# The recurrence's small products of two heads issued as one run per level, into one PSUM bank

## The chip, the cores and the metric

One core of one Trainium2 chip. The metric is the device time of one launch in microseconds; 912.33 us is the median of three runs of the kernel before (911.7, 912.37, 912.33). The engines are named as the profile names them: PE (TensorE, with its weight loads as PEld), DVE (VectorE), ACT (ScalarE), POOL (GpSimd), SP (SyncE, which issues the DMAs).

## The reference

A transformer block on 512 rows of width 1024: one input projection feeds three branches (A: attention over selected keys with a learned bias per distance, B: a gated linear recurrence with 4 heads, C: latent attention), whose outputs are gated, added and projected, and a gated feed-forward layer follows. The change touches branch B alone:

```python
# per head, key width 128, value width 128; f is the gate, k = (1-lb)*sigmoid(-f_raw)
b = cumsum(log f)                      # inside a chunk
decay[t, s] = exp(b[t] - b[s]) for s <= t, else 0
attn[t, s] = sum_k q[t,k] * k[s,k] * decay[t,s,k]
o = attn @ v + (q * exp(b)) @ state
state = exp(b_last) * state + (k * exp(b_last - b)).T @ v
o = rms_norm(o, out_gain) * silu(g)
```

Since the decay depends on the key channel, `attn` is no single product. The kernel builds it by doubling: for two neighbouring blocks of `hh` rows, the later block's queries times the earlier block's keys is one small product, if the queries carry the gates since the start of their block and the keys the gates up to the end of theirs.

## The kernel before

The kernel is written as a list of operations that a planner orders. `Plan.add` (line 167) records each operation with the buffers that it reads and writes; `Plan.run` (232) then walks through a simulated time, gives each engine the operation that can start first (ties go to the one written first), with costs from `Plan.cost` (204), and assigns tiles to buffer slots; `Plan.emit` (319) issues everything in that order. Every instruction therefore has one and the same line, 323, in the profile, and its tile's names tell what it is. Within an engine the order is fixed when the program is built. `SLACK` (26) adds 500 ns in that simulated time before PE takes what another engine made. Work marked `background` (773) is taken only where nothing else is ready: above all the bias of branch A (`bias_unit`, 719), which DVE and ACT build by selecting among leaves (tile `mux`), and its mask (`block_mask`, 757).

The recurrence is `hgrn_pair` (910), called for heads (0, 1) and (2, 3). Per head it holds the queries `qT` (named `qp` in the levels), the keys `kT`, the gates `fT`, the products of neighbouring gates `tt`, the blocks on the diagonal `ac` and the whole 128x128 triangles of four chunks, `at`. First come the 16 products of 32x32 that give the diagonal. Then seven levels, `hh` = 1, 2, ..., 64. Each level, for each head by itself:

- takes a bank of tag `t` (`LIMIT`: three at a time) and issues the level's small products into it: 16 of 32x16 (levels 1 to 16), 8 of 32x32 (level 32) or 4 of 64x64 (level 64). Each product uses a strip of 32 or 64 columns of the array, and its result stands in the matching partitions. An fp32 product shows as two records in the profile;
- merges the result: for `hh` < 32 with a masked copy on DVE into `ac`, for 32 and 64 with copies on ACT into `at`;
- multiplies half of the queries and half of the keys by the level's gates (two DVE products of 128x256), so that the next level can start.

Other work on PE at that time is large products of 128x512 (the next projections: `ps<-hT_hi,whi` and the like), which the planner puts between the runs. After the recurrence come the gates and upward projections of branches C and B (`branch`, 1045, with `oc` and `ob`), then the attention of branch A, which needs the bias.

Of the kernel before, what the change touches and what calls it, by code (L numbers as in the profile page):

```python
# [143 lines left out]
class Plan:  # L144
# [22 lines left out]
    def add(self, choices):  # L167
        op = Op()
        op.choices, op.prio = choices, self.shift + len(self.ops)
        op.deps, op.users, op.ready, op.bufs, op.late = set(), [], 0.0, [], 0  # L170
        _, method, a, k = choices[0]
        args = list(a) + list(k.values())
        outs = [k[n] for n in ("out", "accum_out") if n in k]
        if "out" not in k:
            outs.append(a[0])
        for v in args:
            if not isinstance(v, View):
                continue
            write = any(v is o for o in outs)
            b = v.buf  # L180
            mask = 0
            for i in np.unique(v.idx // 64) if b.cls != "bank" else (0,):
                mask |= 1 << int(i)
            keep = []
            for other, m, w in b.log:
                if m & mask and (write or w) and other is not op:
                    op.deps.add(other)
                if not (write and m | mask == mask):
                    keep.append((other, m, w))
            keep.append((op, mask, write))  # L190
            b.log = keep
            if b not in op.bufs:
                op.bufs.append(b)
                b.left += 1
        if self.gate:
            op.deps.add(self.gate)
        for d in op.deps:
            d.users.append(op)
        op.late = len(op.deps)
        self.ops.append(op)  # L200
        return op

    @staticmethod
    def cost(engine, method, a, k):
        views = [v for v in list(a) + list(k.values()) if isinstance(v, View)]
        if method == "dma_start":
            n = max(v.idx.size for v in views)
            return n * 512 / 360.0
        n = max(v.idx.size for v in views)
        psum = any(v.buf.cls == "bank" for v in views)  # L210
        if engine == "PE":
            rhs = a[2]
            n = rhs.idx.size
            if method == "transpose":
                return 109.0
            if rhs.buf.dt == F32R:
                return n / 2.4 + 3 if n >= 256 else n * 4 / 2.4
            return n * 4 / 2.4
        if engine == "ACT":
            return n / 1.2 + (52 if psum else 93) + 93 * sum(isinstance(k.get(x), View) for x in ("scale", "bias")) + (92 if "accum_out" in k else 0)  # L220
        if engine == "DVE":
            if method == "reciprocal":
                return n * 8 / 0.96 + 68
            one = method in ("tensor_copy", "tensor_scalar") and not psum
            return n / (1.92 if one else 0.96) + 68 + (60 if method == "scalar_tensor_tensor" else 0)
        if method == "tensor_tensor" and k.get("op") == ALU.pow:
            return 165.0 * n + 300
        if method == "tensor_scalar":
            return n * 2.5 + 176 if k["op0"] in (ALU.is_le, ALU.is_equal, ALU.is_ge) else n * 0.832 + 162
        return n * 2.105 + 147  # L230
# [88 lines left out]
    def emit(self, nc):  # L319
        real = {"PE": nc.tensor, "DVE": nc.vector, "ACT": nc.scalar, "Pool": nc.gpsimd, "SP": nc.sync}  # L320
        fix = lambda v: v.real() if isinstance(v, View) else v
        for op, (e, method, a, k) in self.run():
            getattr(real[e], method)(*[fix(v) for v in a], **{n: fix(v) for n, v in k.items()})  # L323


@with_exitstack
def block_kernel(ctx: ExitStack, tc: tile.TileContext, x, positions, w_in, w_up_a, w_up_b, w_up_c, w_out, mla_q_norm,
                 mla_w_qb, mla_kv_norm, mla_w_kvb, hgrn_lb_logits, hgrn_out_norm, rel_bias, attn_norm, ffn_norm,
                 w_ffn_gate, w_ffn_up, w_ffn_down, final_norm, consts_f, consts_i, out):
    nc = tc.nc  # L330
# [5 lines left out]
    plan = Plan(slots)  # L336
# [7 lines left out]
    def g(shape=(128, 512), dt=F32, name="g"):  # L344
        return plan.tile("g", shape[1:], dt, name)
# [228 lines left out]
    ci = const((5, 16), I8, "ci")  # L574
# [332 lines left out]
    rows_group([(src(C_BG, 512), 0)], 512, put5)  # L907
    obT = (o8(name="ob_hi"), o8(name="ob_lo"))

    def hgrn_pair(hs):  # L910
        qp, at, ac, tt_ = {}, {}, {}, {}
        for h in hs:

            at[h] = g((128, 4, 128), name="at")
            P.memset(at[h], 0.0)
            ac[h] = g((128, 4, 32), name="ac")
            pd = bank("t", (128, 4, 32))
            for c in range(4):
                for i in range(4):
                    m = 128 * c + 32 * i  # L920
                    PE.matmul(pd[:, c].part(32 * i, 32 * i + 32), kT[h][:, m:m + 32], qT[h][:, m:m + 32], start=True,
                              stop=True)
            V.tensor_mul(ac[h], pd, id32.to_broadcast([128, 4, 32]))
            qp[h] = qT[h]
            V.tensor_mul(qp[h], qT[h], fT[h])
            tt_[h] = g(name="tt")
            f2 = fT[h].rearrange("p (n two) -> p n two", two=2)
            V.tensor_mul(tt_[h][:, 0:256], f2[:, :, 0], f2[:, :, 1])
            o = 0
            n = 256  # L930
            while n > 4:
                a = tt_[h][:, o:o + n].rearrange("p (n two) -> p n two", two=2)
                V.tensor_mul(tt_[h][:, o + n:o + n + n // 2], a[:, :, 0], a[:, :, 1])
                o += n
                n //= 2
        for lv in range(7):
            hh = 1 << lv
            for h in hs:
                pl = bank("t", (128, 4, 16 if hh < 32 else 64))
                if hh == 64:  # L940
                    for c in range(4):
                        s, m = 64 * (c % 2), 128 * c
                        PE.matmul(pl[:, c].part(s, s + 64), kT[h][:, m:m + 64], qp[h][:, m + 64:m + 128], start=True,
                                  stop=True)
                    for e in range(2):
                        A.copy(at[h][:, e:4:2, 64:128].part(0, 64), pl[:, e:4:2].part(64 * e, 64 * e + 64))
                elif hh == 32:
                    for c in range(4):
                        for s in (0, 64):
                            m = 128 * c + s  # L950
                            PE.matmul(pl[:, c, 0:32].part(s, s + 32), kT[h][:, m:m + 32], qp[h][:, m + 32:m + 64],
                                      start=True, stop=True)
                    for s in (0, 64):
                        A.copy(at[h][:, :, s + 32:s + 64].part(s, s + 32), pl[:, :, 0:32].part(s, s + 32))
                else:
                    for c in range(4):
                        for i in range(4):
                            m = 128 * c + 32 * i
                            q2 = qp[h][:, m:m + 32].rearrange("p (n two e) -> p n two e", two=2, e=hh)[:, :, 1]
                            PE.matmul(pl[:, c].part(32 * i, 32 * i + 32), kT[h][:, m:m + 32], q2, start=True, stop=True)  # L960
                    a2 = ac[h].rearrange("p c (n two e) -> p c n two e", two=2, e=hh)[:, :, :, 1]
                    m2 = ci[:, lv:lv + 1].to_broadcast([128, 4, 16]).rearrange("p c (n e) -> p c n e", e=hh)
                    V.copy_predicated(a2, m2, pl.rearrange("p c (n e) -> p c n e", e=hh))
                    if hh == 16:
                        for i in range(4):
                            ii = slice(32 * i, 32 * i + 32)
                            A.copy(at[h][:, :, ii].part(32 * i, 32 * i + 32), ac[h].part(32 * i, 32 * i + 32))
                if hh == 1:
                    tv = fT[h].rearrange("p (n two) -> p n two", two=2)
                else:  # L970
                    o = 512 - 1024 // hh
                    tv = tt_[h][:, o:o + 512 // hh].rearrange("p (n two) -> p n two", two=2)
                qv = qp[h].rearrange("p (n two e) -> p n two e", two=2, e=hh)
                kv = kT[h].rearrange("p (n two e) -> p n two e", two=2, e=hh)
                nn = 256 // hh
                V.tensor_mul(qv[:, :, 1], qv[:, :, 1], tv[:, :, 0:1].to_broadcast([128, nn, hh]))
                V.tensor_mul(kv[:, :, 0], kv[:, :, 0], tv[:, :, 1:2].to_broadcast([128, nn, hh]))
        for h in hs:
            hc = slice(h * 128, (h + 1) * 128)
            pk = bank("t", (128, 4, 128))  # L980
# [339 lines left out]
```

## Time and profile before

| what | value |
|---|---|
| median of three runs | 912.33 us |
| the profiled execution | 910.3 us |
| its span, first to last instruction | 908.5 us |
| mean granted TensorE clock | 0.995 |
| PE busy | 895.1 us, 99% |
| PEld busy | 777.6 us, 86% |
| DVE busy | 695.6 us, 77% |
| ACT busy | 521.5 us, 57% |

The profiled execution is one launch recorded by the hardware; its span leaves out 1.8 us around the instructions. PE and PEld overlap, as do PE's own records: a large product's record lasts 0.39 us, but the next one starts 0.23 us later. What a product costs is therefore read from one start to the next.

### The profile page before, as it was taken

To read this page: it belongs to the slowest core of one execution; us is meant where nothing else is said; L and a number is where in the kernel's file an instruction comes from. 1 tells how busy PE (TensorE), PEld (TensorE's weight loads), DVE (VectorE), ACT (ScalarE), POOL (GpSimd) and SP (SyncE) were. 2 spreads that over 40 slices of the span, in tenths; PEclk is the share of its full clock that TensorE was granted. 3 is DMA by queue.
4 is the path that set the end of the run, shared out by engine and by line. 5 is a ranking of instruction groups with operands and counts; after the bars stand their busy time and mean duration, and the time that the engine had idled before them with its cause. 6 is when DMAs were issued, how large, how long until landed. Compare 5 with 4: busy or idle time off the path is not lost.

```text
span 908.5 us, 15211 instructions
## 1 busy us (share of the span) xinstructions
PE 895.1 (99%) x5870; PEld 777.6 (86%) x5870; DVE 695.6 (77%) x1428; ACT 521.5 (57%) x985; POOL 20.9 (2%) x31
## 2 busy tenths in 40 slices
PE   7999999999999999999999999999999999999996
PEld 7988878886778888887888879999999999888885
DVE  5576999999999999997353448889998899844205
ACT  7656684496858798977742336554544454533103
POOL 2000000000102000000000000000000000000000
PEclk8999999999999999999999999999999999999999
DMA  8333122331122233143032551323333334643102
GB/s 266 81 93 99 48 70 65 99 92 50 48 72 71 69 115 117 47 139 94 1 103 83 176 172 48 117 70 94 97 115 115 93 94 128 177 138 114 47 1 92
DMA packets 76809, 86.53 MB, mean 95 GB/s; under 512 B 8385, under 2 KB 63809, under 8 KB 76737
## 3 DMA queue, kind: packets, MB, share of 16 engines
q1 hardware_dynamic: 76736, 85.57, 31.2%
q8 instruction: 46, 0.75, 0.3%
q14 instruction: 27, 0.21, 0.1%
HBM read 83.46 MB, written 2.10 MB: 94 GB/s over the span
## 4 chain that ended last, share of the span: by engine, by line
PE 92%; DMA 3%; DVE 2%; ACT 1%; issue 1%; SPq 0%; POOLq 0%; POOL 0%; ACTq 0%
PE ps L323 92%; DMA raw<-in_w_ffn_up 1%; DMA raw<-in_w_in 1%; DVE wlo L323 1%; DMA x2b<-in_x 1%; ACT whi L323 1%; DMA raw<-in_w_out 1%; SPq L323 0%; DVE qpT L323 0%; ACT qpT L323 0%; ACT L323 0%; DVE ckT_lo L323 0%; ACT sm L323 0%; DVE kpo L323 0%; DVE qpr L323 0%
## 5 line engine op out<-in xcount | busy, mean ns | idle before, releaser
L323 DVE TENSOR_TENSOR wlo<-raw,whi 128x1024 fp32r<-128x1024 f32 (+3 forms) x115 | 133.1, 1178 | 66.9 <-ACT whi L323 43.8
L323 ACT CAST whi<-raw 128x1024 fp32r<-128x1024 f32 (+3 forms) x115 | 115.1, 1016 | 91.1 <-PE ps L323 28.0
L323 PE MATMUL ps<-hT_hi,whi 128*128 128x512 f32 x328 | 130.9, 399 | 0.0
L323 PE MATMUL ps<-hT_hi,wlo 128*128 128x512 f32 x328 | 129.9, 397 | 0.0
L323 PE MATMUL ps<-hT_lo,whi 128*128 128x512 f32 x328 | 129.4, 395 | 0.0
L323 ACT ACTIVATE mux<-bucket,rb,rbd 128x512 f32<-128x512 f32 (+1 forms) x161 | 108.3, 743 | 11.0 <-DVE bucket L323 4.7
L323 DVE COPY_PREDICATED mux<-bits,mux 128x512 f32<-128x512 int8 x150 | 104.3, 744 | 0.7 <-ACT mux L323 0.6
L323 PE MATMUL ps<-th,sh 128*128 128x256 f32 x288 | 81.5, 283 | 0.0
L323 PE MATMUL ps<-tl,sh 128*128 128x256 f32 x288 | 81.5, 283 | 0.0
L323 PE MATMUL ps<-th,sl 128*128 128x256 f32 x288 | 81.5, 283 | 0.0
L323 ACT CAST sh<-sf 128x512 fp32r<-128x512 f32 x72 | 44.2, 621 | 51.9 <-DVE sf L323 30.0
L323 PEld LDWEIGHTS ps<-hT_hi,wlo 128*128 128x128 f32 x328 | 61.6, 188 | 12.2
L323 PEld LDWEIGHTS ps<-hT_lo,whi 128*128 128x128 f32 x328 | 61.7, 188 | 12.1
L323 PEld LDWEIGHTS ps<-hT_hi,whi 128*128 128x128 f32 x328 | 61.7, 188 | 12.0
L323 PE MATMUL ps<-whi,ah 128*128 128x512 f32 x176 | 68.5, 389 | 0.0
L323 PE MATMUL ps<-wlo,ah 128*128 128x512 f32 x176 | 68.5, 389 | 0.0
L323 PE MATMUL ps<-whi,al 128*128 128x512 f32 x176 | 68.5, 389 | 0.0
L323 PE MATMUL ps<-h_hi,sl 128*128 128x256 f32 x216 | 61.1, 283 | 0.0
L323 PE MATMUL ps<-h_lo,sh 128*128 128x256 f32 x216 | 61.1, 283 | 0.0
L323 PE MATMUL ps<-h_hi,sh 128*128 128x256 f32 x216 | 61.1, 283 | 0.0
L323 PE MATMUL ps<-whi,hT_hi 128*128 128x512 f32 (+3 forms) x160 | 54.2, 345 | 1.4 <-ACT hT_hi L323 1.4
L323 PEld LDWEIGHTS ps<-th,sh 128*128 128x128 f32 x288 | 55.3, 192 | 0.0
(313 smaller groups left out, 2118.2 us busy)
## 6 DMA issues: line engine op xcount, KB each, us to landing
raw<-in_w_in SPq DMA_DIRECT2D x51, 512.0 KB, 4.2
raw<-in_w_ffn_down SPq DMA_DIRECT2D x22, 512.0 KB, 4.3
raw<-in_w_ffn_gate SPq DMA_DIRECT2D x18, 512.0 KB, 3.7
raw<-in_w_ffn_up SPq DMA_DIRECT2D x18, 512.0 KB, 3.7
raw<-in_w_out SPq DMA_DIRECT2D x8, 512.0 KB, 3.9
raw<-in_w_up_c SPq DMA_DIRECT2D x4, 512.0 KB, 3.6
raw<-in_w_up_b SPq DMA_DIRECT2D x4, 512.0 KB, 3.7
raw<-in_w_up_a SPq DMA_DIRECT2D x4, 512.0 KB, 3.6
```

Source lines behind the costliest of these rows:

```text
L323: getattr(real[e], method)(*[fix(v) for v in a], **{n: fix(v) for n, v in k.items()})
```

## The change

The 16 diagonal products and the first level's of both heads go into one bank as one operation of the planner, and each later level's products of both heads into one bank as one operation. The two heads share one `ac` tile of (8, 32), so the masked copy of a level (and the diagonal's multiplication by the identity) is one DVE instruction for both. The queries get a tile of their own (`qp`) instead of being multiplied in place, because the first run reads both forms. The products of neighbouring gates (`tt`) are built a level at a time, at the end of each level, instead of all at the start. The planner's cost of such an operation is 310 + 9 x (number of products) ns.

```diff
@@ Plan.add, Plan.cost, Plan.emit
-        outs = [k[n] for n in ("out", "accum_out") if n in k]
-        if "out" not in k:
+        outs = [k[n] for n in ("out", "accum_out") if n in k] + k.get("outs", [])
+        args += k.get("outs", [])
+        if "out" not in k and "outs" not in k:
             outs.append(a[0])
...
+        if method == "batch":
+            return 310.0 + 9.0 * len(k["outs"])
...
+            if method == "batch":
+                k["body"](nc, *[fix(v) for v in a], *[fix(v) for v in k["outs"]])
+                continue
@@ hgrn_pair
+    def batch(nc, *v):
+        n = len(v) // 3
+        for i in range(n):
+            nc.tensor.matmul(v[2 * n + i], v[i], v[n + i], start=True, stop=True)
+
     def hgrn_pair(hs):
-        qp, at, ac, tt_ = {}, {}, {}, {}
+        at, tt_, qp = {}, {}, {}
+
+        ac = g((128, 8, 32), name="ac")
         for h in hs:
...
-            ac[h] = g((128, 4, 32), name="ac")
-            pd = bank("t", (128, 4, 32))
-            for c in range(4):
-                for i in range(4):
-                    m = 128 * c + 32 * i
-                    PE.matmul(pd[:, c].part(32 * i, 32 * i + 32), kT[h][:, m:m + 32], qT[h][:, m:m + 32], start=True,
-                              stop=True)
-            V.tensor_mul(ac[h], pd, id32.to_broadcast([128, 4, 32]))
-            qp[h] = qT[h]
+            qp[h] = g(name="qp")
             V.tensor_mul(qp[h], qT[h], fT[h])
...
-            o = 0
-            n = 256
-            while n > 4:
-                a = tt_[h][:, o:o + n].rearrange("p (n two) -> p n two", two=2)
-                V.tensor_mul(tt_[h][:, o + n:o + n + n // 2], a[:, :, 0], a[:, :, 1])
-                o += n
-                n //= 2
+        def strips(width, parts):
+            pl = bank("t", (128, 8, width))
+            l, r, o = [], [], []
+            for e, h in enumerate(hs):
+                for rows, cols, a, b in parts(h):
+                    for c in range(4):
+                        for i, (ka_, qb) in enumerate(zip(a(c), b(c))):
+                            n = rows(c, i)
+                            l.append(ka_)
+                            r.append(qb)
+                            o.append(pl[:, 4 * e + c, cols].part(*n))
+            plan.add([("PE", "batch", l + r, {"outs": o, "body": batch})])
+            return pl
...
         for lv in range(7):
             hh = 1 << lv
-            for h in hs:
-                pl = bank("t", (128, 4, 16 if hh < 32 else 64))
...
+            else:
+                w = 0 if lv else 32
+                first = lambda h: [] if lv else [(quarter, slice(0, 32), chunks(kT[h], 32), chunks(qT[h], 32))]
+                pl = strips(w + 16, lambda h: first(h) + [(quarter, slice(w, w + 16), chunks(kT[h], 32),
+                                                           odd(qp[h], hh))])
+                if not lv:
+                    V.tensor_mul(ac, pl[:, :, 0:32], id32.to_broadcast([128, 8, 32]))
+                a2 = ac.rearrange("p c (n two e) -> p c n two e", two=2, e=hh)[:, :, :, 1]
+                m2 = ci[:, lv:lv + 1].to_broadcast([128, 8, 16]).rearrange("p c (n e) -> p c n e", e=hh)
+                V.copy_predicated(a2, m2, pl[:, :, w:w + 16].rearrange("p c (n e) -> p c n e", e=hh))
+            for n, h in enumerate(hs):
...
                 V.tensor_mul(qv[:, :, 1], qv[:, :, 1], tv[:, :, 0:1].to_broadcast([128, nn, hh]))
                 V.tensor_mul(kv[:, :, 0], kv[:, :, 0], tv[:, :, 1:2].to_broadcast([128, nn, hh]))
+                if 0 < hh < 64:
+                    o, n2 = 512 - 512 // hh, 256 // hh
+                    if n2 > 4:
+                        a = tt_[h][:, o:o + n2].rearrange("p (n two) -> p n two", two=2)
+                        V.tensor_mul(tt_[h][:, o + n2:o + n2 + n2 // 2], a[:, :, 0], a[:, :, 1])
```

Levels 32 and 64 (left out above) go through `strips` in the same way, with the copies on ACT unchanged.

## Rows read from the trace of the kernel before

**Rows 1.** The page's first part: busy us, share of the span, instructions.

```profile
PE 895.1 (99%) x5870; PEld 777.6 (86%) x5870; DVE 695.6 (77%) x1428; ACT 521.5 (57%) x985; POOL 20.9 (2%) x31
```

**Rows 2.** The chain that ended last, its share of the span by engine.

```profile
PE 92%; DMA 3%; DVE 2%; ACT 1%; issue 1%; SPq 0%; POOLq 0%; POOL 0%; ACTq 0%
```

**Rows 3.** Windows: from:to, length, busy us (instructions) per engine, clock, DMA share, GB/s.

```profile
207.29:229.43 22.14, 22.14 (x483) 14.76 (x481) 21.13 (x55) 14.16 (x29) 0.00 (x0) 1.00 0.17 50
300.00:400.00 100.00, 100.00 (x443) 82.76 (x442) 98.18 (x163) 92.70 (x142) 0.00 (x0) 1.00 0.31 95
400.00:415.00 15.00, 15.00 (x68) 12.42 (x67) 14.90 (x30) 8.27 (x11) 0.00 (x0) 1.00 0.20 70
```

**Rows 4.** Groups by shape, PE: the small products. After the bar busy us, mean ns.

```profile
L323 PE MATMUL ps<-qT,kT 128*32 128x16 f32 x640 | 8.9, 185 | 0.0
L323 PE MATMUL ps<-qT,kT 128*32 128x32 f32 x192 | 4.1, 199 | 0.0
L323 PE MATMUL ps<-qT,kT 128*64 128x64 f32 x32 | 1.8, 234 | 0.0
```

**Rows 5.** Timeline of PE around one level's run: start, length, what, records.

```profile
212.06 0.39 PE L323 MATMUL ps<-hT_hi,whi 128*128 128x512 f32 x1
212.28 0.40 PE L323 MATMUL ps<-hT_lo,whi 128*128 128x512 f32 x1
212.52 0.40 PE L323 MATMUL ps<-hT_hi,wlo 128*128 128x512 f32 x1
212.84 0.44 PE L323 MATMUL ps<-qT,kT 128*32 128x16 f32 x32
213.22 0.50 PE L323 MATMUL ps<-hT_hi,whi 128*128 128x512 f32 x1
213.55 0.40 PE L323 MATMUL ps<-hT_lo,whi 128*128 128x512 f32 x1
```

**Rows 6.** Timeline of PE around runs of levels 32 and 64.

```profile
267.05 0.39 PE L323 MATMUL ps<-hT_hi,wlo 128*128 128x512 f32 x1
267.37 0.45 PE L323 MATMUL ps<-qT,kT 128*32 128x32 f32 x16
267.75 0.50 PE L323 MATMUL ps<-hT_hi,whi 128*128 128x512 f32 x1
268.18 0.45 PE L323 MATMUL ps<-qT,kT 128*64 128x64 f32 x8
268.56 0.50 PE L323 MATMUL ps<-hT_lo,whi 128*128 128x512 f32 x1
268.90 0.39 PE L323 MATMUL ps<-hT_hi,wlo 128*128 128x512 f32 x1
```

**Rows 7.** Timeline of PE: two runs with one large product between.

```profile
259.42 0.45 PE L323 MATMUL ps<-qT,kT 128*32 128x16 f32 x32
259.80 0.50 PE L323 MATMUL ps<-hT_hi,wlo 128*128 128x512 f32 x1
260.23 0.45 PE L323 MATMUL ps<-qT,kT 128*32 128x16 f32 x32
```

**Rows 8.** Waits, 205 to 280 us: who for whom, us in total, times, longest.

```profile
PEld ps L323 <- issue: 8.0, 23, 0.4
PEld ps L323 <- DVE kT L323: 0.7, 2, 0.4
```

**Rows 9.** Groups by shape, DVE, 205 to 275 us; last, idle before and its releaser.

```profile
L323 DVE TENSOR_TENSOR qT<-qT,tt 128x256 f32<-128x256 f32 x24 | 10.1, 419 | 0.3 <-PE ps L323 0.2
L323 DVE COPY_PREDICATED ac<-ci,ps 128x64 f32<-128x64 int8 x20 | 5.0, 257 | 2.3 <-PE ps L323 2.0
L323 DVE TENSOR_TENSOR ac<-ps,id 128x128 f32<-128x128 f32 x4 | 1.2, 296 | 0.0
```

**Rows 10.** Timeline of DVE: the last mask added to branch A's bias.

```profile
414.54 0.68 DVE L323 TENSOR_TENSOR mux<-mux,neg 128x512 f32<-128x512 f32 x1
```

**Rows 11.** Timeline of PE: where the attention of branch A takes over.

```profile
420.19 0.49 PE L323 MATMUL ps<-ident,sm 128*128 128x128 f32 x3
```

More of the change, by code (lines that the diff above doesn't have):

```diff
@@ L936, in hgrn_pair, with chunks, odd @@
+        def chunks(v, n, o=0, step=1):
+            return lambda c: [v[:, m:m + n] for m in range(128 * c + o, 128 * c + 128, n * step)]
+        def odd(v, hh):
+            return lambda c: [v[:, m:m + 32].rearrange("p (n two e) -> p n two e", two=2, e=hh)[:, :, 1]
+                              for m in range(128 * c, 128 * c + 128, 32)]
+        quarter = lambda c, i: (32 * i, 32 * i + 32)
         for lv in range(7):
             hh = 1 << lv
-            for h in hs:
-                pl = bank("t", (128, 4, 16 if hh < 32 else 64))
[L940 to L944, printed above, removed]
-                    for e in range(2):
[L946 to L952, printed above, removed]
-                    for s in (0, 64):
[L954 to L967, printed above, removed]
@@ new lines, in hgrn_pair @@
+            if hh == 64:
+                pl = strips(64, lambda h: [(lambda c, i: (64 * (c % 2), 64 * (c % 2) + 64), slice(0, 64),
+                                            chunks(kT[h], 64, 0, 2), chunks(qp[h], 64, 64, 2))])
+                for n, h in enumerate(hs):
+                    for e in range(2):
+                        A.copy(at[h][:, e:4:2, 64:128].part(0, 64), pl[:, 4 * n + e:4 * n + 4:2].part(64 * e, 64 * e + 64))
+            elif hh == 32:
+                pl = strips(64, lambda h: [(lambda c, i: (64 * i, 64 * i + 32), slice(0, 32),
+                                            chunks(kT[h], 32, 0, 2), chunks(qp[h], 32, 32, 2))])
+                for n, h in enumerate(hs):
+                    for s in (0, 64):
+                        A.copy(at[h][:, :, s + 32:s + 64].part(s, s + 32), pl[:, 4 * n:4 * n + 4, 0:32].part(s, s + 32))
+            else:
[8 more added lines that the diff above has]
+                V.copy_predicated(a2, m2, pl[:, :, w:w + 16].rearrange("p c (n e) -> p c n e", e=hh))
@@ L968, in hgrn_pair @@
+            for n, h in enumerate(hs):
+                if hh == 16:
+                    for i in range(4):
+                        ii = slice(32 * i, 32 * i + 32)
+                        A.copy(at[h][:, :, ii].part(32 * i, 32 * i + 32), ac[:, 4 * n:4 * n + 4].part(32 * i, 32 * i + 32))
                 if hh == 1:
```

## The prediction

> **What bounds the kernel now.** First the shares: PE is busy 99% of the span [rows 1], and the chain that ended last is PE for 92% [rows 2]. A busy PE says little by itself, so the second look is at windows. The reader is to see the PE column equal to the length of the stretch: all of 22.14 us where the first pair's recurrence runs, all of the 100 us from 300 to 400, all of the 15 us after [rows 3]. In these stretches PE always has a next instruction, so what shortens PE's own stream shortens the kernel, as long as nobody else becomes late. The third look is at the small products. They have 864 records [rows 4], which is 432 products with two records each; per pair of heads they are 2 diagonals and 7 levels for 2 heads, so 16 runs, 32 runs in all. The groups' busy times, 8.9 + 4.1 + 1.8 = 14.8 us, leave out what surrounds a run; the price has to be read from starts.
>
> **One run's price.** Large products start 0.23 us apart (212.06 to 212.52, two steps). From 212.52, the last large product before a run, to 213.55, the second after it, are 1.03 us [rows 5]. Two large steps are 0.46, so the run costs 0.57 us. Where it goes: the first small product starts 0.32 after the large one instead of 0.23; the run's starts spread over 0.44 less one record's own 0.185, so 0.26 us for 31 steps, 8.3 ns each; PE leaves it 0.12 after its last start; and the first large product behind it is followed after 0.33 to 0.34 instead of 0.23. More than half is paid at the two ends. The short runs show it too: one of 16 records and one of 8 with one large product between them take from 267.05 to 268.90, 1.85 us, less three large steps 1.16, 0.58 each [rows 6], though the second has a quarter of the records of a level run. Their steps are longer, (0.45 - 0.20)/15 = 16.7 ns and (0.45 - 0.23)/7 = 31 ns. As a check, the window of the first pair holds 424 small records and about 58 large products that start in it: 22.14 - 58 x 0.23 = 8.8 us for 15 runs, 0.59 each [rows 3].
>
> **What is removed and added on PE.** Per pair the 16 runs become 7: the diagonals and the first level of both heads one run of 128 records, levels 2 to 16 four runs of 64, level 32 one of 32, level 64 one of 16. The count of products is the same. By steps: 0.57 + 96 x 0.0083 = 1.37; 4 x (0.57 + 32 x 0.0083) = 3.34; 0.58 + 16 x 0.0167 = 0.85; 0.58 + 8 x 0.031 = 0.83. Together 6.4 us, where 16 runs took 9.2 to 9.3. Two pairs: 2 x 2.85 = **5.7 us off PE's stream**. The unknown here is the step beyond the 32nd record of a run, since no run before is longer. Taking 8.3 ns I choose the nearest row; the slow end is the first rival.
>
> **DVE and ACT.** Ten masked copies of 128x64 pairs and two of `ac` multiplications become half as many with twice the elements: 12 instructions fewer. The step from 128x128 to 128x256 is 296 to 419 ns, so one twice as long saves at most 2 x 296 - 419 = 173 ns, and for the copies no more than their 257 [rows 9]: between 0 and 3 us, I take 1. The products with the gates, those of neighbouring gates and ACT's copies are the same in number; the latter products only move to the ends of levels, into DVE's stream between the same neighbours, without a DMA or another queue. The extra tile for the queries is paid by the shared `ac` and by `qT`, which is free after the first run. No DMA is added or moved past another; SP's order stays.
>
> **The wait that changes.** Before, a head's run waited for that head's two DVE products while the other head's were under way; now a run waits for all four, and DVE's next products wait for the end of the whole run, because they overwrite what it reads. PE has large products to fill this: its true waits at the recurrence are 0.7 us in two for `kT`, and the 8.0 us in 23 with no releaser are the runs' own entries [rows 8]. DVE's waits for such a run were 2.0 us [rows 9]; with a run of 0.84 instead of 0.57 us, and the planner's 310 + 9 x 32 = 598 ns for it, the filling that the planner picks is short by 0.24 a level. Twelve levels: up to 3 us more of idle DVE, at least none. It hits no PE work there, since two pairs' later projections and all of branch C's gates stand behind.
>
> **What is late next.** Branch A's bias is the other long work: from 300 to 400 us DVE is busy 98.18 and ACT 92.70 of 100, from 400 to 415 DVE 14.90 of 15 [rows 3]. Its last mask is added at 414.54 + 0.68 = 415.2 [rows 10], and PE turns to that attention at 420.19 [rows 11]. So PE can come 5.0 us earlier before it meets unfinished bias; it will come 5.7 earlier. DVE's own end moves by -1 to +3 us. What is lost there lies between 0 and all 5.7; early blocks of that attention and gates of branch A can fill, so I take 1.0. Net 4.7. Against the profiled execution: 910.3 - 4.7 = 905.6; the median of the runs lies 2.0 above that execution, so the forecast is **907.6 us**. Its own range is 905.5 to 910.
>
> **Rival 1, slower: long runs starve.** Until 32 records everything of a run may stand ready in PE before it begins; beyond, instructions have to be brought in while it runs. The rows allow a slow rate: from 259.42 two runs with one large product end their starts at 260.23 + 0.26, 1.07 us [rows 7]. If the first 32 were ready, the 33 behind them came in at 32 ns each or faster. Beyond the 32nd record lie 96 + 4 x 32 = 224 per pair, 448 in all. At 32 ns these cost 448 x (32 - 8.3) = 10.6 us more, less 5.7: 912.3 + 4.9 = **917.2 us**. It turns the sign from 8.3 + 5700/448 = 21 ns. For it: nothing shows a longer run. Against it: two runs so close together cost 0.58 each as well [rows 6], and a run with 8 records as much as one with 32, so no supply limit shows yet.
>
> The Trainium skill has a rule on this side ("TensorE: Matmul & The Clock Gate", section "Wait — 56ns, not 53.3ns?"): however small a product, the next one starts no less than about 25 ns later. Worked out from that figure, 32 more records would cost 0.80 us, more than the 0.57 that a run's ends and body cost, and the estimate for the change would be about 2 us slower. Inside a run this trace shows 8.3 ns, since neighbouring products use different strips, so the page's floor does not hold there; beyond the 32nd record no run here shows it.
>
> **Rival 2, no change: the bias holds it up.** PE arrives early at an attention whose bias isn't ready, and stands until it is. For it: the slack of 5.0 us is smaller than the gain, and DVE and ACT have no air for 100 us. Against it: PE has filled every such place so far. If DVE ends 1 us later and nothing fills, PE gains 5.0 - 1 = 4.0 less the way of the first blocks through DVE and ACT, which is 3 to 4 us of the present 5.0: some 0.5 us stay, **911.8**.
>
> **Rival 3: PE waits inside the runs.** If at each of the 12 later runs the fourth DVE product is late by its own 0.42 us [rows 9], PE loses 12 x 0.42 = 5.0 and the sum is 912.3 - 5.7 + 5.0 = **911.6**. Against it: PE is slower than the planner assumes (0.23 for a large product charged at 216 ns), so DVE tends to be early.
>
> **Chances.** Forecast 0.60; rival 1 0.16, of which some part would be a smaller loss or even a small gain; rival 2 0.14; rival 3 0.05; a new order that moves some other wait, either way, 0.05. About 0.2% of the time, 1.8 us, can be told from no change. Faster: the forecast, and the weak forms of rivals 1 and 3 and of the new order, 0.71. Same: rivals 2 and 3 in the main, 0.14. Slower: rival 1 and the rest, 0.15. The range reaches from 904.5 (all of 5.7, DVE's relief and 1 us of luck) to 914.0, which takes in rivals 2 and 3 and rival 1 with a step of some 25 ns; a full rival 1 is left out.
>
> **What would show it.** Right: 14 runs with 128, 64, 32 and 16 records; a run of 64 with starts spread over some 0.53 us; 0.84 us from large product to large product for it, above the two steps; from the first run to the last of a pair about the same time as before with more large products in it; PE full from 200 to 420. Rival 1: steps that lengthen behind the 32nd record. Rival 2: PE idle, or waiting for `sm` or `pT`, where the attention of branch A starts, with DVE's last mask close to 415. Rival 3: waits of PE for `qp` or `kT` at most runs. The forecast is wrong if PE's small work falls by 5 to 6 us and the time doesn't follow, or if it doesn't fall.

## The result, and the profile after

The changed kernel takes **906.91 us** (median of four, 906.78 to 907.51) against 912.35 for the kernel before on the same chip: a ratio of 0.9942, with a 95% interval from 0.9925 to 0.9959, or 5.4 us. The forecast was 907.6. Medians here and below leave out one slow execution, of the changed kernel with half of the background work, which took 2282.09 us.

The page of the changed kernel, its busy times:

```profile
PE 890.4 (98%) x5870; PEld 778.1 (86%) x5870; DVE 694.4 (77%) x1417; ACT 520.3 (57%) x983; POOL 19.7 (2%) x31
```

PE's records are 5870 as before, and it is busy 4.7 us less [rows 1]. Its span is 905.0 us against 908.5: 3.5 shorter, so PE stands 1.2 us longer than before. The windows show where (columns as in [rows 3]):

```profile
212.04:235.43 23.39, 23.39 (x494) 18.31 (x493) 20.10 (x53) 13.28 (x27) 0.00 (x0) 1.00 0.33 92
300.00:400.00 100.00, 100.00 (x443) 82.65 (x442) 97.52 (x161) 81.54 (x121) 0.00 (x0) 1.00 0.33 97
400.00:415.00 15.00, 15.00 (x70) 12.40 (x68) 15.00 (x27) 11.65 (x21) 0.00 (x0) 1.00 0.24 69
415.00:451.00 36.00, 34.77 (x204) 28.11 (x203) 21.26 (x85) 30.09 (x74) 0.00 (x0) 1.00 0.17 55
```

The reader is to see the last line: 34.77 of 36.00, the only stretch from 200 to 500 us in which PE isn't full. The first line is the first pair's recurrence up to its last run: 494 records, of which 416 small in six runs and some 77 large that start in it, so 23.39 - 77 x 0.23 = 5.7 us for six runs; before, 15 runs took 8.8 in [rows 3].

One level's run, PE's timeline (start, length, what, records), to be held against [rows 5]:

```profile
216.44 0.39 PE L329 MATMUL ps<-hT_hi,wlo 128*128 128x512 f32 x1
216.76 0.74 PE L919 MATMUL ps<-qp,kT 128*32 128x16 f32 x64
217.43 0.50 PE L329 MATMUL ps<-hT_hi,whi 128*128 128x512 f32 x1
217.76 0.39 PE L329 MATMUL ps<-hT_lo,whi 128*128 128x512 f32 x1
```

From 216.44 to 217.76 are 1.32 us, less two large steps 0.86. The entry is 0.32 and the step behind the first large product 0.33, as before; only the middle is longer, (0.74 - 0.185)/63 = 8.8 ns a record. The first run of a pair, its inner lines left out:

```profile
212.04 0.39 PE L329 MATMUL ps<-hT_lo,whi 128*128 128x512 f32 x1
212.36 0.46 PE L919 MATMUL ps<-qT,kT 128*32 128x32 f32 x32
...
213.21 0.43 PE L919 MATMUL ps<-qp,kT 128*32 128x16 f32 x30
213.57 0.50 PE L329 MATMUL ps<-hT_hi,wlo 128*128 128x512 f32 x1
213.91 0.39 PE L329 MATMUL ps<-hT_hi,whi 128*128 128x512 f32 x1
```

128 records cost 1.87 - 0.46 = 1.41 us. DVE in the recurrence, its groups by shape and then its longest waits:

```profile
L329 DVE COPY_PREDICATED ac<-ci,ps 128x128 f32<-128x128 int8 x10 | 3.6, 359 | 1.8 <-PE ps L919 1.7
L329 DVE TENSOR_TENSOR ac<-ps,id 128x256 f32<-128x256 f32 x2 | 0.8, 420 | 0.5 <-PE ps L919 0.5
```

```profile
DVE qp L329 <- PE ps L919: 2.5, 2, 1.8
DVE ac L329 <- PE ps L919: 2.2, 5, 0.9
```

A copy for both heads takes 359 ns where two took 2 x 257. The waits for runs add up to 4.7 us, against the 2.2 of [rows 9]. Of the 2.5 more, 1.8 are one wait, at the last level of the first pair.

Where PE stands, its timeline with the idle time in brackets:

```profile
420.18 0.39 PE L329 MATMUL ps<-hT_hi,wlo 128*128 128x512 f32 x1
421.80 0.33 PE L329 MATMUL ps<-ident,sm 128*128 128x128 f32 x1 [1.23 <-ACT sm L329]
```

And the chain of waits that leads there, in order of time (start, us, what):

```profile
411.85 1.11 DVE wlo L329
412.96 0.02 issue
412.98 5.05 DMA raw<-in_w_in
418.03 0.02 issue
418.05 0.02 ACT whi L329
418.07 1.04 issue
419.12 1.28 ACT L329
420.41 1.34 ACT sm L329 x5
```

DVE, busy 97% and more since 300 us, frees a buffer for raw weights at 412.96; the next load of the gates' weights takes it and lands 5.05 us later; ACT, which works in order, has the cast of these weights (`whi`) in front, then loads its function table (1.28 us), and only then comes the attention's first exponential (`sm`), for which PE stands.

### The profile page after: what moved, and what is told of

It reads as the page before. It is cut to its first block, busy times and chain, and to the rows that moved or that the text cites. A ratio compares the mean times of both kernels' runs of the same rounds, so it can differ in the third digit from the quotient of the medians.

```text
span 905.0 us, 15189 instructions
## 1 busy us (share of the span) xinstructions
PE 890.4 (98%) x5870; PEld 778.1 (86%) x5870; DVE 694.4 (77%) x1417; ACT 520.3 (57%) x983; POOL 19.7 (2%) x31
## 4 chain that ended last, share of the span: by engine, by line
PE 90%; DMA 3%; DVE 3%; ACT 2%; issue 1%; SPq 0%; POOLq 0%; POOL 0%; ACTq 0%; DVEq 0%
PE ps L329 89%; DMA raw<-in_w_in 1%; PE ps L919 1%; DVE wlo L329 1%; DMA x2b<-in_x 1%; DMA raw<-in_w_ffn_up 1%; DVE mux L329 1%; ACT whi L329 1%; DMA raw<-in_w_out 0%; SPq L329 0%; ACT L329 0%; ACT sm L329 0%; DVE qpT L329 0%; ACT qpT L329 0%; ACT sg L329 0%
```

## The experiments

Each was timed beside the kernel before, which lay at 912.05 to 912.43 us.

**Every small product twice.** The result is written twice; the order on PE, DVE and ACT is the same.

```diff
+        for _ in range(2):
             for i in range(n):
                 nc.tensor.matmul(v[2 * n + i], v[i], v[n + i], start=True, stop=True)
```

> The changed kernel in which every small product of a run is issued twice, the same result twice; the order of the plan is unchanged. Theory (a run costs its two ends once, and 8.7 ns per record of a 32-wide strip): the ends stay, 864 records come on top, per pair 128 x 8.7 + 256 x 8.7 + 32 x 16.2 + 16 x 31 = 4.4 us, so 8.7 us more, 906.9 + 8.7 = 915.6, or as low as 914.4 if PE's 1.2 us of standing at 421 us closes. Steps stay at 8.7 ns in runs of 128 and 256 records. Rival (long runs starve): steps lengthen behind some record, at 25 ns 864 x 25 = 22 us more, 928. Rival (the price goes by the product, not by the run): the runs' 13 us double, 920.

Measured: 925.71 us, ratio 1.0149 (1.0135 to 1.0163), 18.8 above the changed kernel: far above the theory and the second rival, and below the 928 of the first. A level's run of 128 keeps the theory's step, (1.27 - 0.185)/127 = 8.5 ns:

```profile
231.80 0.39 PE L329 MATMUL ps<-hT_hi,whi 128*128 128x512 f32 x1
232.12 1.27 PE L920 MATMUL ps<-qp,kT 128*32 128x16 f32 x128
233.32 0.50 PE L329 MATMUL ps<-hT_lo,whi 128*128 128x512 f32 x1
233.66 0.40 PE L329 MATMUL ps<-hT_hi,wlo 128*128 128x512 f32 x1
```

But the pair's first run, now 256 records, stops some 235 records in. PE's timeline, its waits on itself, and the windows around (the number before DMA's share is the granted clock):

```profile
213.94 0.25 PE L920 MATMUL ps<-qp,kT 128*32 128x16 f32 x9
217.53 0.51 PE L920 MATMUL ps<-qp,kT 128*32 128x16 f32 x21 [3.34 <-issue]
217.97 0.80 PE L329 MATMUL ps<-hT_hi,wlo 128*128 128x512 f32 x1
218.56 0.63 PE L329 MATMUL ps<-hT_hi,whi 128*128 128x512 f32 x1
218.99 0.63 PE L329 MATMUL ps<-hT_lo,whi 128*128 128x512 f32 x1
```

```profile
PE ps L920 <- issue: 6.0, 3, 3.3
```

```profile
212.00:214.20 2.20, 2.19 (x236) 2.08 (x236) 0.90 (x2) 0.04 (x1) 0.00 (x0) 1.00 0.92 249
214.20:217.50 3.30, 0.00 (x0) 0.00 (x0) 0.00 (x0) 1.48 (x2) 0.00 (x0) 0.82 0.44 145
217.50:220.00 2.50, 2.48 (x26) 2.05 (x26) 1.92 (x6) 0.00 (x0) 0.00 (x0) 0.50 0.03 7
220.00:223.00 3.00, 3.00 (x9) 2.33 (x8) 1.77 (x5) 1.64 (x3) 0.00 (x0) 0.50 0.00 0
```

No engine releases the pause ("issue"), PE's weight loads stop with it, and the second pair's first run pauses likewise, for 2.2 us, but only before the last of its 256 records; a level's run of 128 pauses for 0.45. The three pauses take 6.0 us. In the longest one PE does nothing, and behind it the granted clock is 0.50 (1.2 GHz) up to 223 us; behind the second it is 0.50 from 261 to 264. So the first rival's starving exists, but as a stop far behind the 32nd record, not as a slower step. The rest of the excess, 18.8 less 8.7 and 6.0, is about what the low clock costs: large products start 0.43 us apart there instead of 0.23, and the 21 steps behind the two long pauses take 8.9 us where 4.9 would do.

**Twice, but not the first run of a pair.** No run has over 128 records.

```diff
+        for _ in range(1 if n == 64 else 2):
```

> As the kernel with every product issued twice, but the first run of a pair (128 records) once: no run has more than 128 records. There the two runs of 256 records stopped for 3.3 and 2.2 us in their middle. Theory (a step costs 8.7 ns, and only a run of some 230 records or more outruns the supply of instructions): per pair 256 x 8.7 + 32 x 16.2 + 16 x 31 = 3.25 us, 6.5 in all, 913.4, no pause of over 0.7 us inside a run. Rival (the extra time of the kernel with all products twice lies in all long runs alike): half of its 18.8 us and more, over 916.

Measured: 914.54 us, ratio 1.0025 (1.0016 to 1.0034), 7.6 above the changed kernel where 6.5 were expected. The difference is in a row of waits:

```profile
PE ps L920 <- issue: 1.3, 4, 0.4
```

Four runs of 128 pause for 0.2 to 0.4 us each, which is about the 1.1 us beyond the expected 6.5. Three of them start 4 to 5 us after the run before, one, the second pair's first run, some 10; four other runs of 128 that start 4 to 6 us after one don't pause. So neither a run's length nor its distance from the last decides it alone; what the trace shows of it stands in the last section. In the changed kernel no run pauses.

**Runs broken in the middle.** One full-width product of 16 columns after half of a run, into columns that the run overwrites.

```diff
+            if i == n // 2:
+                nc.tensor.matmul(wide[2], wide[0], wide[1], start=True, stop=True)
             nc.tensor.matmul(v[2 * n + i], v[i], v[n + i], start=True, stop=True)
```

> The changed kernel in which one full-width product (128x128 stationary, 16 columns, into columns that the run overwrites later) stands in the middle of each of the 14 runs; the plan's order is unchanged but for the planner's 9 ns. Theory (the ends cost): each break costs a run's two ends again, 0.32 us, and some 0.05 for the product: 14 x 0.37 = 5.2 us, 912.1, or 910.9 if PE's standing closes. Rival (the price goes by the product): 14 x 0.05 = 0.7 us, 907.6.

Measured: 912.1 us, ratio 0.9996 (0.9986 to 1.0006): 14 products of 16 columns give back the whole gain. The timeline of a level's run:

```profile
217.47 0.39 PE L329 MATMUL ps<-hT_hi,wlo 128*128 128x512 f32 x1
217.79 0.45 PE L922 MATMUL ps<-qp,kT 128*32 128x16 f32 x32
218.17 0.40 PE L921 MATMUL ps<-kT 128*128 128x16 f32 x2
218.49 0.45 PE L922 MATMUL ps<-qp,kT 128*32 128x16 f32 x32
218.87 0.50 PE L329 MATMUL ps<-hT_hi,whi 128*128 128x512 f32 x1
219.20 0.39 PE L329 MATMUL ps<-hT_lo,whi 128*128 128x512 f32 x1
```

1.73 us less two large steps is 1.27, where the unbroken run cost 0.86: 0.41 for a break, 14 x 0.41 = 5.7. The number of strip products, the merged work on DVE and the order on every engine are those of the changed kernel, so none of these makes the gain. The price lies where strips and full-width products meet; what there makes it was not taken apart.

**One head per run**, 28 runs, the diagonal still merged.

```diff
-        def strips(width, parts):
-            pl = bank("t", (128, 8, width))
+        def strips(width, parts, hs):
+            pl = bank("t", (128, 4, width))
...
+            for n, h in enumerate(hs):
...
+                    pl = strips(w + 16, lambda h: first(h) + [(quarter, slice(w, w + 16), chunks(kT[h], 32),
+                                                               odd(qp[h], hh))], (h,))
```

> The changed kernel with one run per head and level, each into a bank of its own, the diagonal still merged with the first level: 28 runs instead of 14. Theory (the ends cost): 14 x 0.32 = 4.5 us more, 911.4, or 910.2 if PE's standing closes. Rival (the gain comes from the plan's new order, the operation of the planner and its lower cost): about 907.

Measured: 910.34 us, ratio 0.9977 (0.9967 to 0.9987). PE stands nowhere in its attention of branch A here, which is the theory's lower case. The time falls with the number of runs, though this kernel also has DVE's copies for each head by itself.

**The planner's operation alone**: the kernel before, its 32 runs each one operation with the new cost.

```diff
-                            PE.matmul(pl[:, c].part(32 * i, 32 * i + 32), kT[h][:, m:m + 32], q2, start=True, stop=True)
+                            items.append((pl[:, c].part(32 * i, 32 * i + 32), kT[h][:, m:m + 32], q2))
+                    run_of(items)
```

> The kernel before with its 32 runs as they are, each made one operation of the planner with the cost 310 + 9 x products: the new kind of operation alone. Theory (the ends cost): 912.3, within 0.8. Rival (the gain comes from the plan's new order): 907 to 908.

Measured: 912.32 us, ratio 1.0003 (0.9995 to 1.0012). By themselves the new kind of operation and its cost gain nothing that can be told from noise, about 1 us.

**A fourth buffer for raw weights**, in the changed kernel and in the one before.

```diff
-    for cls, n in (("st", 24), ("raw", 3), ("big", 10), ("hT", 2), ("g", NG), ("bank", 8)):
+    for cls, n in (("st", 24), ("raw", 4), ("big", 10), ("hT", 2), ("g", NG), ("bank", 8)):
```

> The changed kernel with four buffers for raw weights instead of three. In the changed kernel PE stands for 1.23 us at 420.6, because ACT waits for a weight load that could only start when DVE had freed its buffer, with the attention's exponentials queued behind it. Theory (that chain takes the missing part of the gain): the load starts earlier, PE doesn't stand there, 905.7 (906.9 - 1.2), with 0.5 either way from a new order. Rival (the unfinished bias holds it, as the prediction's second rival says): PE stands there still, 906.9.

> The kernel before with four buffers for raw weights: control for the changed kernel with four. PE stood nowhere in its attention of branch A, so both theories expect 912.3, within 0.7; if it gains 1.2 us as well, four buffers help by another way than the one named.

Measured: the changed kernel 903.84 us, ratio 0.9908 (0.9895 to 0.9922), the best of all; the kernel before 912.44, ratio 0.9998 (0.9988 to 1.0007). The changed kernel with four buffers, its window of that attention and its busy times:

```profile
415.00:451.00 36.00, 36.00 (x212) 29.64 (x211) 22.14 (x85) 30.73 (x75) 0.00 (x0) 1.00 0.16 53
```

```profile
PE 889.1 (99%) x5870; PEld 777.8 (86%) x5870; DVE 694.7 (77%) x1419; ACT 516.8 (57%) x981; POOL 16.9 (2%) x31
```

PE is full there, as the chain said. The gain is 3.1 us and not 1.2: a stand of 0.73 us near 527, at the output projection, is gone too, and PE is busy 1.3 less; which part of the new order does the latter is open. The buffer does change the order: DVE's differs from its 49th instruction on. The control is not clean: in the kernel before with four buffers PE newly stands for 1.6 us inside the second recurrence and 0.6 at 390, so it can't say what the buffers alone are worth there.

**The run's measured cost in the planner**, alone and with four buffers.

```diff
-            return 310.0 + 9.0 * len(k["outs"])
+            w = a[0].idx.size
+            return 310.0 + (17.5, 32.0, 62.0)[(w > 32) + (k["outs"][0].idx.size == 32 and len(k["outs"]) == 16 or w > 32)] * len(k["outs"])
```

> The changed kernel with the planner's cost of a run as measured (310 + 17.5 per product of the 32-wide strips, 32 at level 32, 62 at level 64: 1.43, 0.87, 0.82, 0.81 us) instead of 310 + 9: only the order can change. Theory (the order around the attention sets up to 1.2 us): between 905.7 and 907.5. Rival (the gain of the change came from the planner's too low cost): it goes back toward 912.

> The changed kernel with four raw buffers and the measured cost of a run in the planner. Theory: the buffers close PE's standing, the cost only reorders: 903.8, within 1. Rival (each of the two gains by itself): 903.3 or less.

Measured: 906.6 us, ratio 0.9942 (0.9929 to 0.9956), and with four buffers 905.46, ratio 0.9925 (0.9912 to 0.9938). A truer cost is worth nothing by itself that can be told from noise. It too closes the stand in the attention (PE is busy all of the 36.00 us), but PE then stands for 0.4 us at 273 and for 0.7 us more than the changed kernel from 500 to 600. With four buffers it loses 1.6 us, against the expectation: PE stands for 0.4 and 0.3 us at 275 and 291, and the rest was not taken apart.

**Half of the background work**, to take DVE's and ACT's backlog away.

```diff
-            for k in range(16):
+            for k in range(8):
                 leaf = plan.tile("g", (per, n), F32, "mux", tag="mux" if k else "g")
```

> The kernel before with 8 instead of 16 leaves in each selection of branch A's bias (so the bias is another one): about half of the background work on DVE and ACT is gone. PE is full in either case: 912, at most 1 less.

> The changed kernel with 8 leaves as well. Theory (PE's stream is 5.6 us shorter, and the rest of the gain is held up only by DVE's and ACT's backlog before the attention): no standing of PE there, 5.6 us or a little more below the kernel before with 8 leaves, so about 906. Rival (PE's standing there is in the order of the work, not in the backlog): it stands as long as with 16 leaves, about 907.

Measured: 913.13 us before, above the expected 912, ratio 1.0007 (0.9998 to 1.0017), and 906.91 changed (median of four), ratio 0.9940 (0.9926 to 0.9954): 6.2 between them. The windows of the changed kernel with half the leaves:

```profile
300.00:400.00 100.00, 100.00 (x443) 82.69 (x442) 60.31 (x104) 39.06 (x56) 0.00 (x0) 1.00 0.34 105
...
415.00:451.00 36.00, 36.00 (x214) 29.87 (x213) 17.71 (x72) 28.84 (x72) 0.00 (x0) 1.00 0.11 31
```

With DVE at 60% PE is full through the attention: with half of the background work, and the order that comes with it, there is no stand. Its worth in time can't be read from these medians, since 6.2 and 5.4 differ by less than their intervals, and the changed kernel takes 906.91 with the full background work as well.

## Why the prediction was right

- **One run's price** held: 0.57 us with more than half at the two ends. The broken runs show it directly, and the kernels with 32, 28 and 14 runs lie at 912.3, 910.3 and 906.9 us.
- **PE's stream, 5.7 us.** By the runs' own rows 1.41 + 4 x 0.86 + 0.83 + 0.81 = 6.5 per pair instead of 6.4, so 2 x (9.25 - 6.5) = 5.5 us. The step beyond the 32nd record was taken as 8.3 ns and is 8.8.
- **DVE's relief**, taken as 1 us of at most 3, is 10 x (2 x 257 - 359) + 2 x (2 x 296 - 420) = 1.9 us.
- **The wait that changes**, given up to 3 us of more idle DVE, cost 4.7 - 2.2 = 2.5. The size lies in the range, but it came otherwise: not as a filling short by 0.24 us at each of twelve levels, but as one wait of 1.8 us in the main.
- **What is late next** had the right place and size, 1.0 us forecast and 1.23 measured, but the wrong cause, so that the size fits is luck. The prediction feared an unfinished bias, and let DVE's end move by 3 us at most. In the changed kernel DVE adds the last mask only at 430.83:

```profile
430.83 0.69 DVE L329 TENSOR_TENSOR mux<-mux,neg 128x512 f32<-128x512 f32 x1
```

That is 16 us later than in [rows 10], and PE does not stand for it: the planner puts early blocks of the attention first. PE stands for an exponential behind a weight cast that waits for a load. With half of the background work the stand is gone, so the backlog has a part in it. That the buffer is the link is what the chain says, and the fourth buffer agrees with it; but that run has a new order, and the measured cost closes the stand with three buffers, so the buffer is not shown to be the only way.
- **Rival 1** (starving) holds beyond the lengths used here; its bound of 32 ns a record was far too high up to 128 records (8.5 to 8.8 ns), and it is a stop rather than a step. **Rival 3** (waits inside the runs) did not occur: only one of 14 runs enters later than the rest, by 0.1 us.
- **The sum.** Net 4.7 was forecast, 5.4 is the difference of the medians, and 3.5 that of the two profiled spans. The changed kernel's profiled execution reaches one and the same wait at 122 us 0.9 us later than the one before, ahead of all that changed; that is about half of what the two numbers differ by. That it comes from the first loads of that execution is argued, not shown. From that wait to the end the span is 4.4 us shorter (786.7 to 782.3), which is what the terms make as measured: 5.5 less 1.2 is 4.3. The remaining 1.0 us of the medians' 5.4 is not explained, so 907.6 against 906.9 is closer than the terms deserve.

## What to carry to other kernels

Read the price of a small group of products from the start of the large product before it to the start of the second one after it, not from its busy time: here 0.3 of 0.57 us lies at the ends, and merging groups pays as often as it removes ends. When PE's stream gets shorter, follow the next stand back along its chain to a resource that is cheap to add; a fourth buffer for raw weights gave a further 3 us in the changed kernel, with a new order, and nothing in the one before. Don't lengthen such runs without limit, since both runs of 256 small records stopped for 2 to 3 us in their course.

## What the runs showed of the hardware

A run of small products that use neighbouring strips keeps 8.5 to 8.8 ns a record up to 128 records (256 instructions with the weight loads). With 256 it stopped for 3.3 us behind 235 records and for 2.2 us behind 255, and of the ten runs of 128 in the kernel with the later products twice four stopped for 0.2 to 0.4 us, others not.

The trace suggests what decides it. Its instruction queue moves pieces of 16 KB: 46 in the changed kernel, 53 and 51 in the two kernels with products twice, which is one for every 254 or 255 records of PE and PEld together. All seven pauses of these two kernels stand at one place in this count, 193 or 194 records beyond a multiple of 256. Call such a place a border; a run of 128 crosses one, a run of 256 two. At each pause PE goes on 1.2 to 1.4 us after a piece has landed (the longest stop ends at 217.53 us, its piece moved from 215.32 to 216.26). In the runs of 128 that don't pause, the last piece had landed 2.0 us or more before the border. When a piece comes depends on other traffic: in the kernel with the later products twice, three of the four pauses follow a piece that started 2.2 to 2.9 us after the border before, while weight loads kept the DMA engines 76 to 89% busy; in four runs without a pause it started after 0.9 to 1.1 us, with the DMA engines idle. Two of these stretches, the late one ahead of the pause at 232 us (DMA share in the second last column):

```profile
226.67:229.55 2.88, 2.88 (x92) 2.46 (x81) 2.88 (x8) 0.00 (x0) 0.00 (x0) 1.00 0.76 196
222.60:223.47 0.87, 0.87 (x72) 0.80 (x61) 0.23 (x2) 0.87 (x2) 0.00 (x0) 1.00 0.00 0
```

The fourth pause has only 1.6 us between two borders. That PE waits for its instructions, and that weight loads hold these up, is read from this agreement; no run here moved a piece or a load.
